# Scores of the banded layers: two heads side by side in the two halves of TensorE's rows

## The chip, the cores and the metric

The kernel runs on one core of a Trainium2 chip, as one launch. The metric is the device time of that core in microseconds (us). The engines are named as in the profile: PE is TensorE's matmul, PEld its weight load, DVE VectorE, ACT ScalarE, POOL GpSimd, SP SyncE, which issues most DMAs. L12 is line 12 of the kernel.

## The reference

A stack of four layers on 1024 image tokens and 256 context tokens of width 1024: windowed attention, latent attention, a gated recurrence, and windowed attention again. The change touches the two layers with windowed attention (0 and 3, here "banded"). There 16 query heads of 64 dimensions share 4 key heads; a block of 128 queries sees three blocks of 128 keys round it and all 256 context keys:

```python
logits = jnp.einsum('bqkgd,bjkd->bkgqj', q_b, k_b).astype(jnp.float32) * scale
p = sink_softmax(jnp.where(mask, logits, NEG_INF), sink_l)
return jnp.einsum('bkgqj,bjkd->bqkgd', p.astype(v_b.dtype), v_b)
```

Context queries (layer 0 alone) see the context keys only. Inputs and outputs are float32.

## The kernel before

To keep float32 accuracy at the rate of the rounded type float32r, each operand is split into a rounded part ("hi") and the rest ("lo"), and products of parts are summed in PSUM. Projections take three products (hi hi, hi lo, lo hi).

A banded layer (`layer_a`) first makes keys and values, then works through units: a group g of four heads that share a key head, by a tile t of 128 queries, 40 units in layer 0 (2 context tiles and 8 image tiles a group) and 32 in layer 3. Queries and keys lie in DRAM (`qd`, `kd`) as four slabs: even and odd dimensions (32 rows each) of hi, and the same of lo. `load_group` (L862) fetches for a group the keys, the four slabs stacked to 128 rows (tile `ks`, 128 x 1280), and the values. `load_q` (L870 to 878) fetches a unit's queries twice: stacked in the same order, and with hi and lo exchanged (tile `qT`, 128 x 2 x 4 x 128). A score product over 128 rows with the first copy gives hi hi + lo lo, with the second hi lo + lo hi.

`stage_s` (L898 to 932) makes the scores of a unit. For each of the four heads it takes a PSUM tile `w` (two buffers), multiplies queries (weights, 128 x 128) with image keys (384 columns, 256 at the two edge tiles, none for context tiles) and with 256 context keys, two products each. Then POOL puts the sink in, DVE adds the mask and takes the maximum (L921), ACT takes the exponential (L923), and for two heads together DVE inverts the sums and POOL scales (L928, L930). `fill(n)` lets n matmuls of the projections of later heads (generator `pq`) follow each head. `stage_pv` (L934 on) turns the probabilities of the unit before with PE transposes (L90), splits them and multiplies them with the values; at its end the result is multiplied with the gate `zin` on POOL (L966) and written out. `made_for` draws the projections that a load needs. `proj_z` makes the gates by way of tile `zs`.

All matmuls go through `mm` (L87), so their lines are one; the tile names tell them apart: `w<-ks,qT` are the scores, `n<-hh,wzh` and the like projections, `n<-ph,v` and `n<-pl,v` the value products, `n<-raw,cs` the conditioning vectors of the next layer, four tiles of 32 columns of the array side by side.

Each engine runs its queue in order. The order in a queue isn't the program's: the framework's scheduler sorts instructions by priority (place in the program) and by when a simulated timeline finds them ready, with waits put in for buffers.

Of the kernel before, what the change touches and what calls it, by code (L numbers as in the profile page):

```python
# [9 lines left out]
F32 = mybir.dt.float32  # L10
F32R = mybir.dt.float32r
BF16 = mybir.dt.bfloat16  # L12
AF = mybir.ActivationFunctionType
ALU = mybir.AluOpType
# [5 lines left out]
NLAT = 1024  # L20
NCTX = 256
T = NLAT + NCTX
# [9 lines left out]
def as32(ap):  # L32
    return ap.bitcast(F32)
# [31 lines left out]
class Dit:  # L65
# [652 lines left out]
    def layer_a(self, i, hpool, hT, hs):  # L718
        nc, ins, P = self.nc, self.ins, self.P
# [3 lines left out]
        qd = [self.pd.tile([4, 128, T], F32, name=f"qd{i}_{g}") for g in range(4)]  # L723
        kd = self.pd.tile([4, 128, T], F32, name=f"kd{i}")
# [29 lines left out]
        for n, t in enumerate(self.order(i - 1)):  # L754
            norm[1](n + 2)
            ps = self.psn()
# [10 lines left out]
            if n == 1:  # L767
                self.run_late()
                qp = self.pool("qp", hs)
# [17 lines left out]
        p2 = self.pool("p2", os_)  # L787
        mask = p2.tile([128, 1152], BF16, name="mask")
        nsink = p2.tile([128, 16], F32, name="nsink")
# [3 lines left out]
        p3 = self.pool("p3", os_)  # L793
# [4 lines left out]
        def piece(w, c, t0, m):  # L798

            hh, hl = hT  # L800
            ps = self.psn()
            ts = slice(t0, t0 + m)
            for k in range(8):
                for x, (a_, b_) in enumerate(((w.wh, hh), (w.wh, hl), (w.wl, hh))):
                    self.mm(ps[:, 0:m], a_[:, k, c], b_[:, k, ts], k == 0 and x == 0, k == 7 and x == 2)
                    yield ps
# [14 lines left out]
        def proj_z(x, pieces):  # L821

            w = P["z", x]
            for t0, m in pieces:
                for ps in piece(w, slice(0, 128), t0, m):
                    yield
                zs = qp.tile([128, 512], F32, name="zs", bufs=2)
                nc.scalar.activation(out=zs[:, 0:m], in_=ps[:, 0:m], func=AF.Tanh, scale=0.5)
                nc.vector.scalar_tensor_tensor(out=zs[:, 0:m], in0=zs[:, 0:m], scalar=1.0, in1=ps[:, 0:m],
                                               op0=ALU.add, op1=ALU.mult)  # L830
                nc.sync.dma_start(out=zd[x * 128:(x + 1) * 128, t0:t0 + m], in_=zs[:, 0:m])
                made.add(("z", x, t0))
# [17 lines left out]
        def made_for(kind, xs, t):  # L850

            for x in xs:
                while (kind, x, t * 128 // 512 * 512) not in made:
                    next(pq)


        fs, fp = (5, 5, 5, 2), (2, 2, 2, 2, 1)
# [2 lines left out]
        st = {}  # L860

        def load_group(g):  # L862
            ks = p2.tile([128, T], F32R, name="ks", bufs=2)
            for p in range(4):
                nc.sync.dma_start(out=as32(ks[32 * p:32 * p + 32]), in_=kd[p, 32 * g:32 * g + 32, :])
            v2 = p2.tile([128, NT, 128], F32R, name="v2", bufs=2)
            nc.sync.dma_start(out=as32(v2), in_=vd[g].rearrange("(t p) d -> p t d", p=128))
            grp[g] = (ks, v2)

        def load_q(u):  # L870
            g, t = units[u]
            made_for("q", (g,), t)
            q = p2.tile([128, 2, 4, 128], F32R, name="qT", bufs=2)
            for x in range(2):
                for p in range(4):
                    nc.sync.dma_start(out=as32(q[32 * p:32 * p + 32, x]),
                                      in_=qd[g][(p + 2 * x) % 4, :, t * 128:(t + 1) * 128].rearrange("(h i) t -> i h t", i=32))
            st[u] = {"qT": q}

        def load_z(u):  # L880
            g, t = units[u]
            made_for("z", (2 * g, 2 * g + 1), t)
            z = p2.tile([128, 2, 128], F32, name="zin", bufs=2)
            nc.sync.dma_start(out=z, in_=zd[g * 256:(g + 1) * 256, t * 128:(t + 1) * 128]
                              .rearrange("(a p) t -> p a t", p=128))
            st[u]["z"] = z
# [11 lines left out]
        def stage_s(u, fill):  # L898
            g, t = units[u]
            qT = st[u]["qT"]  # L900
            ks = grp[g][0]
            s0, mo, kbs = cols(t)
            n = 768 - s0
            nl = 512 - s0
            lsum = p3.tile([128, 4], F32, name="lsum", bufs=2)
            nm = p3.tile([128, 4], F32, name="nm", bufs=2)
            rl = p3.tile([128, 4], F32, name="rl", bufs=2)
            pr = []
            for j in range(4):
                ps = self.psw()  # L910
                if nl:
                    kk = slice(kbs[0] * 128, kbs[0] * 128 + nl)
                    for x in range(2):
                        self.mm(ps[:, s0:512], qT[:, x, j, :], ks[:, kk], x == 0, x == 1)
                for x in range(2):
                    self.mm(ps[:, 512:768], qT[:, x, j, :], ks[:, NLAT:T], x == 0, x == 1)
                p = p3.tile([128, 641], F32, name="p", bufs=8)
                sink = nsink[:, 4 * g + j:4 * g + j + 1]
                nc.gpsimd.tensor_scalar(out=p[:, n:n + 1], in0=sink, scalar1=1.0, scalar2=1.0, op0=ALU.mult, op1=ALU.mult)

                nc.vector.tensor_tensor_reduce(out=p[:, 0:n], in0=ps[:, s0:768], in1=mask[:, mo:mo + n], scale=1.0,  # L921
                                               scalar=sink, op0=ALU.add, op1=ALU.min, accum_out=nm[:, j:j + 1])
                nc.scalar.activation(out=p[:, 0:n + 1], in_=p[:, 0:n + 1], func=AF.Exp, scale=-1.0, bias=nm[:, j:j + 1],  # L923
                                     accum_out=lsum[:, j:j + 1])
                pr.append(p)
                fill(fs[j])
                if j % 2:
                    nc.vector.reciprocal(out=rl[:, j - 1:j + 1], in_=lsum[:, j - 1:j + 1])  # L928
                    for y in (j - 1, j):
                        nc.gpsimd.tensor_scalar(out=pr[y][:, 0:n], in0=pr[y][:, 0:n], scalar1=rl[:, y:y + 1], scalar2=0.5,  # L930
                                                op0=ALU.mult, op1=ALU.mult)
            st[u].update(pr=pr, kbs=kbs)

        def stage_pv(u, fill, end=False):  # L934
            g, t = units[u]
            pr, kbs = st[u]["pr"], st[u]["kbs"]
            load_z(u)
            v2 = grp[g][1]
            po = self.psn()
            nk = len(kbs)  # L940
            prev = None

            def pv(b, ph, pl):
                self.mm(po, v2[:, kbs[b], :], ph, b == 0, False)
                self.mm(po, v2[:, kbs[b], :], pl, False, b == nk - 1)

            for b in range(nk):
                pt = self.psn()
                for j in range(4):
                    self.tr(pt[:, j * 128:(j + 1) * 128], pr[j][:, b * 128:(b + 1) * 128])  # L950
                ph = p3.tile([128, 512], F32R, name="ph", bufs=2)
                pl = p3.tile([128, 512], F32R, name="pl", bufs=2)
                self.split(ph, pl, pt, "act", "dve")
                fill(1 if end else fp[b])
                if prev:
                    pv(*prev)
                prev = (b, ph, pl)
            pv(*prev)
            up = p3.tile([64, 512], F32, name="up", bufs=1)
            nc.scalar.activation(out=up, in_=po[64:128, :], func=AF.Copy)  # L960
            o = p3.tile([128, 2, 128], F32, name="o", bufs=2)
            pv_ = po[0:64, :].rearrange("p (a b t) -> p b a t", b=2, t=128)
            uv = up[:, :].rearrange("p (a b t) -> p b a t", b=2, t=128)
            for b in range(2):
                nc.vector.tensor_tensor(out=o[64 * b:64 * b + 64], in0=pv_[:, b], in1=uv[:, b], op=ALU.add)
            nc.gpsimd.tensor_tensor(out=o, in0=o, in1=st[u]["z"], op=ALU.mult)  # L966
            nc.sync.dma_start(out=od[g * 256:(g + 1) * 256, t * 128:(t + 1) * 128]
                              .rearrange("(a p) t -> p a t", p=128), in_=o)
            del st[u]

        load_group(0)
        made_for("q", (0,), qtiles[-1])
        made_for("z", (0,), qtiles[-1])
        load_q(0)
        load_q(1)
        nu = len(units)
        nq = len(qtiles)
# [4 lines left out]
        def fill(n):  # L982
            for _ in range(n):
                next(pq, None)
        early = 3 if i == self.depth - 1 else 1
        last = nu - 7
        for s in range(nu + 1):
# [20 lines left out]
            if s == nu - early:  # L1008
# [5 lines left out]
                fs, fp = (4, 3, 3, 0), (0, 2, 0, 0, 0)  # L1014
# [1073 lines left out]
```

## Time and profile before

| | us |
|---|---|
| median of 3 runs | 3014.71 (3012.68 to 3015.23) |
| the profiled execution | 3015.6 |
| its span, first to last instruction | 3013.8 |
| PE busy in it | 2825.1 (94%) |
| DVE, POOL, ACT busy | 1631.5, 1297.6, 1246.6 |
| first banded layer's units | about 167 to 640 |
| last banded layer's units | about 2532 to 2935 |

Busy time of PE is the time in which at least one matmul is under way by the profile. A matmul's length there holds its way through the array, so that consecutive ones overlap: what one costs is the distance from its start to the next start. The timeline joins like instructions that follow one another (x8) and gives the first one's start. Its columns are start, length, engine, line, operation, output and inputs, rows*columns of the array, shape, count, and in brackets the idle time before with what ended it.

### The profile page before, as it was taken

What the parts mean: (1) busy time and instruction counts of PE and PEld (TensorE: products, weight loads), DVE (VectorE), ACT (ScalarE), POOL (GpSimd) and SP (SyncE); (2) the same over time, 40 slices, a digit from 0 to 9 for tenths busy, and PEclk for the clock granted to TensorE, in tenths of its full rate; (3) what the DMA queues carried; (4) which work ended last, traced back from release to release, by engine and by line L of the source; (5) the groups of instructions that cost most, each with busy time, mean ns of one, the idle gap of its engine ahead of it and who ended that gap; (6) DMA issues with size and microseconds to landing.
All of it is one profiled execution on the core that took longest, in us unless ns stands there. A gap on an engine that the chain in (4) does not pass through costs nothing. (4 is left out here: it accounts for less than half of the span.)

```text
span 3013.8 us, 49186 instructions
## 1 busy us (share of the span) xinstructions
PE 2825.1 (94%) x17272; PEld 2450.8 (81%) x17272; DVE 1631.5 (54%) x3491; ACT 1246.6 (41%) x2625; POOL 1297.6 (43%) x1543
## 2 busy tenths in 40 slices
PE   6999999899999999999899999998997989999898
PEld 4888888678877788888787788998896788888777
DVE  5356666555522566666456644444465743666662
ACT  2245555543311455555433323331233422555662
POOL 4555555545661011000454231345554536656652
PEclk9999999999999999999999999999999999999999
DMA  8455463644255211111443443997686546444433
GB/s 269 146 164 158 139 177 113 216 121 133 80 193 174 75 37 36 34 36 33 128 141 114 136 146 122 301 290 246 225 274 231 186 126 185 123 117 140 146 101 111
DMA packets 460856, 446.33 MB, mean 148 GB/s; under 512 B 39394, under 2 KB 394234, under 8 KB 460610
## 3 DMA queue, kind: packets, MB, share of 16 engines
q1 hardware_dynamic: 456016, 440.40, 47.1%
q8 instruction: 137, 2.24, 0.3%
q10 hardware_dynamic: 4162, 2.14, 0.3%
q0 software_dynamic: 432, 0.66, 0.1%
q14 instruction: 109, 0.89, 0.1%
HBM read 308.19 MB, written 135.53 MB: 147 GB/s over the span
## 5 line engine op out<-in xcount | busy, mean ns | idle before, releaser
L104 DVE TENSOR_TENSOR pl<-n,ph 128x512 fp32r<-128x512 f32 x488 | 327.5, 686 | 135.8 <-ACT ph L95 117.7
L95 ACT ACTIVATE ph<-n 128x512 fp32r<-128x512 f32 x488 | 284.3, 597 | 214.6 <-PE n L90 169.4
L87 PE MATMUL n<-ph,v 128*128 128x256 f32 (+1 forms) x992 | 293.1, 338 | 22.6 <-ACT ph L95 16.8
L921 DVE CUSTOM_DVE_ANT_0 p<-w,mask,nsink 128x640 f32<-128x640 f32 (+2 forms) x288 | 225.0, 806 | 145.1 <-PE w L87 106.4
L87 PE MATMUL n<-wh,hh 128*128 128x256 f32 x960 | 281.6, 294 | 19.7 <-DVE sg L1752 13.4
L90 PE MATMUL n<-ident,p 128*128 128x128 f32 x1952 | 291.9, 276 | 3.4 <-DVE eo_t L290 1.2
L87 PE MATMUL n<-wl,hh 128*128 128x256 f32 x960 | 278.6, 290 | 2.3 <-DVE wl L104 2.3
L923 ACT ACTIVATE p<-p,nm 128x641 f32<-128x641 f32 (+2 forms) x288 | 220.8, 768 | 139.1 <-DVE nm L921 112.1
L87 PE MATMUL n<-wh,hl 128*128 128x256 f32 x960 | 278.0, 290 | 0.0
L90 PEld LDWEIGHTS n<-ident,p 128*128 128x128 f32 x1952 | 236.9, 143 | 37.3 <-ACT p L1288 2.8
L930 POOL TENSOR_SCALAR p<-p,rl 128x640 f32<-128x640 f32 (+2 forms) x288 | 212.0, 749 | 114.8 <-DVE rl L928 111.2
L87 PE MATMUL n<-pl,v 128*128 128x512 f32 (+1 forms) x656 | 238.1, 363 | 7.8 <-DVE pl L104 6.8
L1339 POOL TENSOR_TENSOR o<-o,z 128x256 f32<-128x256 f32 x40 | 30.4, 759 | 438.6 <-ACT o L1338 235.1
L87 PEld LDWEIGHTS n<-wh,hh 128*128 128x128 f32 x960 | 190.1, 198 | 25.3 <-DVE sg L1752 15.0
L87 PEld LDWEIGHTS n<-ph,v 128*128 128x128 f32 x992 | 175.1, 190 | 42.4 <-ACT ph L95 26.5
L87 PE MATMUL w<-ks,qT 128*128 128x256 f32 (+1 forms) x1088 | 197.9, 308 | 1.5 <-DMA qT<-qd 0.7
L87 PEld LDWEIGHTS n<-wl,hh 128*128 128x128 f32 x960 | 190.2, 198 | 3.3 <-DVE wl L104 3.0
L87 PEld LDWEIGHTS n<-wh,hl 128*128 128x128 f32 x960 | 190.1, 198 | 0.3
L87 PEld LDWEIGHTS w<-ks,qT 128*128 128x128 f32 x1088 | 173.3, 189 | 18.6 <-DVE nm L921 5.2
L104 POOL TENSOR_TENSOR wl<-raw,wh 128x1024 fp32r<-128x1024 f32 x42 | 106.3, 2535 | 117.3 <-DVE wh L97 98.5
L87 PEld LDWEIGHTS n<-pl,v 128*128 128x128 f32 x656 | 125.0, 191 | 26.4 <-DVE pl L104 18.4
L87 PE MATMUL n<-hh,wh 128*128 128x512 f32 (+1 forms) x336 | 123.6, 368 | 5.9 <-DVE mod L402 5.9
(341 smaller groups left out, 7312.0 us busy)
## 6 DMA issues: line engine op xcount, KB each, us to landing
raw<-in_l_w_ada_dram SPq DMA_DIRECT2D x96, 512.0 KB
raw<-in_l_w_in_dram SPq DMA_DIRECT2D x80, 512.0 KB
qT<-qd SPq DMA_DIRECT2D x576, 64.0 KB
raw<-in_l_w_out_dram SPq DMA_DIRECT2D x32, 512.0 KB
vd<-v SPq DMA_DIRECT2D x60, 256.0 KB
xd<-xt SPq DMA_DIRECT2D x30, 512.0 KB
od<-o SPq DMA_DIRECT2D x112, 128.0 KB
go<-od SPq DMA_DIRECT2D x28, 512.0 KB
```

The costliest lines, as they stand in the source:

```text
L87: self.nc.tensor.matmul(out, lhsT, rhs, start=start, stop=stop)
L90: self.nc.tensor.transpose(out, in_, self.ident)
L95: nc.scalar.activation(out=out, in_=in_, func=AF.Copy)
L104: e.tensor_tensor(out=lo, in0=src, in1=as32(hi), op=ALU.subtract)
L921: nc.vector.tensor_tensor_reduce(out=p[:, 0:n], in0=ps[:, s0:768], in1=mask[:, mo:mo + n], scale=1.0, scalar=sink, op0=ALU.add, op1=ALU.mi ...
L923: nc.scalar.activation(out=p[:, 0:n + 1], in_=p[:, 0:n + 1], func=AF.Exp, scale=-1.0, bias=nm[:, j:j + 1], accum_out=lsum[:, j:j + 1])
L930: nc.gpsimd.tensor_scalar(out=pr[y][:, 0:n], in0=pr[y][:, 0:n], scalar1=rl[:, y:y + 1], scalar2=0.5, op0=ALU.mult, op1=ALU.mult)
L1339: nc.gpsimd.tensor_tensor(out=o, in0=o, in1=z, op=ALU.mult)
```

## The change

`stage_s` takes the heads in pairs and both `w` buffers at once. Each head has 64 rows of the array (even and odd dimensions of one part), the first of the pair rows 0 to 63, the second rows 64 to 127, and takes three products (hi hi, hi lo, lo hi) for each stretch of keys, in turn with the other head's; lo lo is left out. `load_q` puts the second head of a pair into the upper 64 rows and fetches each part once. `load_group` puts the keys' hi and lo side by side and the same keys into both halves, so `ks` doubles. To make room, `zs`, `zin` and `o` have one buffer instead of two.

```diff
-                zs = qp.tile([128, 512], F32, name="zs", bufs=2)
+                zs = qp.tile([128, 512], F32, name="zs", bufs=1)
...
-            ks = p2.tile([128, T], F32R, name="ks", bufs=2)
-            for p in range(4):
-                nc.sync.dma_start(out=as32(ks[32 * p:32 * p + 32]), in_=kd[p, 32 * g:32 * g + 32, :])
+            ks = p2.tile([128, 2, T], F32R, name="ks", bufs=2)
+            for y in range(2):
+                for b in range(2):
+                    nc.sync.dma_start(out=as32(ks[64 * y + 32 * b:64 * y + 32 * b + 32]),
+                                      in_=kd[b::2, 32 * g:32 * g + 32, :].rearrange("x i t -> i x t"))
...
-            q = p2.tile([128, 2, 4, 128], F32R, name="qT", bufs=2)
-            for x in range(2):
-                for p in range(4):
-                    nc.sync.dma_start(out=as32(q[32 * p:32 * p + 32, x]),
-                                      in_=qd[g][(p + 2 * x) % 4, :, t * 128:(t + 1) * 128].rearrange("(h i) t -> i h t", i=32))
+            q = p2.tile([128, 2, 2, 128], F32R, name="qT", bufs=2)
+            for y in range(2):
+                for b in range(2):
+                    for x in range(2):
+                        nc.sync.dma_start(out=as32(q[64 * y + 32 * b:64 * y + 32 * b + 32, x]),
+                                          in_=qd[g][b + 2 * x, :, t * 128:(t + 1) * 128]
+                                          .rearrange("(h y i) t -> y i h t", y=2, i=32)[y])
...
-            z = p2.tile([128, 2, 128], F32, name="zin", bufs=2)
+            z = p2.tile([128, 2, 128], F32, name="zin", bufs=1)
...
-            for j in range(4):
-                ps = self.psw()
-                if nl:
-                    kk = slice(kbs[0] * 128, kbs[0] * 128 + nl)
-                    for x in range(2):
-                        self.mm(ps[:, s0:512], qT[:, x, j, :], ks[:, kk], x == 0, x == 1)
-                for x in range(2):
-                    self.mm(ps[:, 512:768], qT[:, x, j, :], ks[:, NLAT:T], x == 0, x == 1)
...
+            for j0 in (0, 2):
+                pss = [self.psw() for _ in range(2)]
+                parts = [(s0, 512, kbs[0] * 128)] if nl else []
+                for c0, c1, k0 in parts + [(512, 768, NLAT)]:
+                    kk = slice(k0, k0 + c1 - c0)
+                    for x, (a, b) in enumerate(((0, 0), (0, 1), (1, 0))):
+                        for y in range(2):
+                            r = slice(64 * y, 64 * y + 64)
+                            self.mm(pss[y][:, c0:c1], qT[r, a, j0 // 2, :], ks[r, b, kk], x == 0, x == 2)
+                for y in range(2):
+                    j = j0 + y
...
+                    fill(fs[j])
+                nc.vector.reciprocal(out=rl[:, j0:j0 + 2], in_=lsum[:, j0:j0 + 2])
...
-            o = p3.tile([128, 2, 128], F32, name="o", bufs=2)
+            o = p3.tile([128, 2, 128], F32, name="o", bufs=1)
```

## Rows read from the trace of the kernel before

**Rows 1.** The page's first part: busy time, share of the span, instructions.

```profile
PE 2825.1 (94%) x17272; PEld 2450.8 (81%) x17272; DVE 1631.5 (54%) x3491; ACT 1246.6 (41%) x2625; POOL 1297.6 (43%) x1543
```

**Rows 2.** Stretches: from:to, length, busy us of PE, PEld, DVE, ACT, POOL; clock, DMA.

```profile
166.00:560.00 394.00, 388.58 (x2390) 333.14 (x2383) 249.57 (x606) 222.44 (x488) 224.74 (x354) 1.00 0.50 149
560.00:640.00 80.00, 66.71 (x409) 50.75 (x408) 49.31 (x121) 47.45 (x93) 46.17 (x65) 0.86 0.67 206
...
2840.00:2935.00 95.00, 81.70 (x444) 66.93 (x443) 61.49 (x137) 63.87 (x128) 61.45 (x88) 0.96 0.46 136
```

**Rows 3.** Timeline of PE: start us, length us (first to last end), instruction, xcount.

```profile
356.68 1.34 PE L87 MATMUL w<-ks,qT 128*128 128x384 f32 x8
357.85 0.60 PE L90 MATMUL n<-ident,p 128*128 128x128 f32 x4
```

**Rows 4.** Groups by shape, whole span, PE: xcount, busy us, mean ns, idle, releasers.

```profile
L87 PE MATMUL w<-ks,qT 128*128 128x256 f32 x704 | 134.1, 285 | 0.8 <-DMA qT<-qd 0.4 <-DVE nm L921 0.3
...
L87 PE MATMUL w<-ks,qT 128*128 128x384 f32 x384 | 104.5, 351 | 0.7 <-DMA qT<-qd 0.2 <-DVE nm L921 0.2
```

**Rows 5.** Timeline of PE round tiles of 32 columns in the first banded layer.

```profile
277.41 0.39 PE L87 MATMUL n<-hh,wql 128*128 128x512 f32 x1
277.63 0.39 PE L87 MATMUL n<-hh,wqh 128*128 128x512 f32 x1
277.95 0.64 PE L87 MATMUL n<-raw,cs 128*32 128x256 f32 x8
278.52 0.50 PE L87 MATMUL n<-hl,wqh 128*128 128x512 f32 x1
278.86 0.40 PE L87 MATMUL n<-hh,wql 128*128 128x512 f32 x1
```

**Rows 6.** Timeline of the weight loads (PEld) in the same stretch.

```profile
277.95 0.16 PEld L87 LDWEIGHTS n<-raw,cs 128*32 128x32 f32 x8 [0.35 <-issue]
278.52 0.19 PEld L87 LDWEIGHTS n<-hl,wqh 128*128 128x128 f32 x1 [0.41 <-issue]
```

**Rows 7.** Timeline of PE round sixteen tiles of 32 columns.

```profile
413.55 1.07 PE L87 MATMUL n<-raw,cs 128*32 128x256 f32 x16
414.55 0.50 PE L87 MATMUL w<-ks,qT 128*128 128x256 f32 x2
```

**Rows 8.** Groups by shape, whole span, weight loads (PEld).

```profile
L87 PEld LDWEIGHTS w<-ks,qT 128*128 128x128 f32 x1088 | 173.3, 189 | 18.6 <-DVE nm L921 5.2 <-issue 1.5 <-DVE eo_t L289 0.4
...
L87 PEld LDWEIGHTS n<-raw,cs 128*32 128x32 f32 x768 | 20.0, 116 | 41.7 <-DMA raw<-in_l_w_ada_dram 15.0 <-issue 14.7 <-DVE eo_t L303 1.7
```

**Rows 9.** Timeline of PE round a transpose of 36 rows, third layer.

```profile
1877.71 0.27 PE L90 MATMUL n<-ident,s 128*128 128x128 f32 x1
1877.92 0.25 PE L1620 MATMUL n<-ident,s 36*128 36x36 f32 x1
1878.10 0.39 PE L87 MATMUL n<-wh,hh 128*128 128x256 f32 x1
1878.32 0.28 PE L87 MATMUL n<-wl,hh 128*128 128x256 f32 x1
1878.43 0.28 PE L87 MATMUL n<-wh,hl 128*128 128x256 f32 x1
```

**Rows 10.** Timeline of PE: the first and the last interrupted run of a head.

```profile
185.78 0.84 PE L87 MATMUL w<-ks,qT 128*128 128x256 f32 x5
186.47 0.40 PE L87 MATMUL n<-pl,v 128*128 128x512 f32 x1
186.70 0.51 PE L87 MATMUL w<-ks,qT 128*128 128x256 f32 x3
...
2927.79 0.52 PE L87 MATMUL w<-ks,qT 128*128 128x256 f32 x3
...
2928.38 0.28 PE L87 MATMUL w<-ks,qT 128*128 128x256 f32 x1
```

**Rows 11.** Tile zin: what ended its engine's idle time (us, times).

```profile
  DMA zin<-zd: 5.1, 2
```

More of the change, by code (lines that the diff above doesn't have):

```diff
@@ L908, in stage_s @@
             pr = []
-            for j in range(4):
-                ps = self.psw()
-                if nl:
-                    kk = slice(kbs[0] * 128, kbs[0] * 128 + nl)
-                    for x in range(2):
-                        self.mm(ps[:, s0:512], qT[:, x, j, :], ks[:, kk], x == 0, x == 1)
-                for x in range(2):
-                    self.mm(ps[:, 512:768], qT[:, x, j, :], ks[:, NLAT:T], x == 0, x == 1)
[L917 to L931, printed above, removed]
@@ new lines, in stage_s @@
+            for j0 in (0, 2):
[9 more added lines that the diff above has]
+                    j = j0 + y
+                    p = p3.tile([128, 641], F32, name="p", bufs=8)
+                    sink = nsink[:, 4 * g + j:4 * g + j + 1]
+                    nc.gpsimd.tensor_scalar(out=p[:, n:n + 1], in0=sink, scalar1=1.0, scalar2=1.0, op0=ALU.mult,
+                                            op1=ALU.mult)
+                    nc.vector.tensor_tensor_reduce(out=p[:, 0:n], in0=pss[y][:, s0:768], in1=mask[:, mo:mo + n], scale=1.0,
+                                                   scalar=sink, op0=ALU.add, op1=ALU.min, accum_out=nm[:, j:j + 1])
+                    nc.scalar.activation(out=p[:, 0:n + 1], in_=p[:, 0:n + 1], func=AF.Exp, scale=-1.0,
+                                         bias=nm[:, j:j + 1], accum_out=lsum[:, j:j + 1])
+                    pr.append(p)
+                    fill(fs[j])
+                nc.vector.reciprocal(out=rl[:, j0:j0 + 2], in_=lsum[:, j0:j0 + 2])
+                for y in (j0, j0 + 1):
+                    nc.gpsimd.tensor_scalar(out=pr[y][:, 0:n], in0=pr[y][:, 0:n], scalar1=rl[:, y:y + 1], scalar2=0.5,
+                                            op0=ALU.mult, op1=ALU.mult)
```

## The prediction

> **What bounds the kernel now.** I read the page's first part first: TensorE is busy for 94% of the span and no other engine for more than 54% [rows 1]. Busy time alone does not say that it streams, since matmuls overlap, so the second view is the table by stage: in the main stretch of the first banded layer PE is busy for 388.6 of 394 us, while at the two ends, where the projections that fill its gaps have run out, it is idle for 13.3 of 80 us and 13.3 of 95 us [rows 2]. The third is the pace inside the score products. Eight of them, two heads of 4 x (384+256) columns, follow one another from 356.68 to 357.85, 1.17 us for 2560 columns, 0.457 ns a column, with the next weights loaded meanwhile [rows 3]. The clock is at its upper level, 2.4 GHz (granted 1.00), in this stretch [rows 2]. So a banded layer is bound by how long TensorE's own sequence takes, and what the change does to that sequence is nearly all of its price. The fourth view counts what it touches: 704 score products of 256 columns and 384 of 384 columns [rows 4], 704x256 + 384x384 = 327,680 columns, 149.8 us at 0.457 ns.
>
> **Part 1: fewer columns in time.** Before, a head takes two full-array products for each stretch of keys; after, three products of 64 rows, and two heads lie in the two halves of the rows. If both halves stream at once, two heads need 3 column passes where they needed 4: 149.8 x 3/4 = 112.4 us, a gain of **37.4 us**. The trace has no two products in different rows, so this is not shown; what it has is four 32-column tiles side by side: eight such products with a whole visit of the mode take 0.57 us and sixteen take 1.00 us [rows 5, 7], hence 0.43 us for eight more, 0.215 us for four of 256 columns together. A 512-column product at the same place takes 0.23 us (277.41 to 277.63) [rows 5]. Tiles beside one another in columns do run together, and I take the same for rows.
>
> **Part 2: going in and out of the half-height mode.** Every other product round these uses the whole array, so each unbroken run of the new products is entered and left once. The trace shows what such a visit costs, in two places. (a) Tiles of 32 columns: the 512-column product starts at 277.63, the tiles at 277.95, 0.32 us later instead of 0.23: 0.09 us of draining. The weight load starts only then, not ahead (277.95, after 0.35 us idle, put down to issue) [rows 5, 6]. On the way out the load again starts with its product at 278.52, and the product after that comes at 278.86, 0.34 us later instead of 0.23: 0.11 us for a load of 128 columns that nothing hides [rows 5, 6]. In all 277.63 to 278.86 is 1.23 us, of which two products of 0.23 and two groups of 0.215 are work: the visit costs 1.23 - 0.46 - 0.43 = 0.34 us. Its loads on the way in have 32 columns, 116 ns each, where the new ones have 128 columns, 189 ns [rows 8]; 0.07 us more is exposed, **0.41 us**. (b) A transpose of 36 rows among full-height work, which is the same kind of step: transpose, 36-row transpose and two 256-column products take from 1877.71 to 1878.43, 0.72 us, where four steps of the neighbours' 0.12 us would be 0.48: **0.24 us**, with ten such transposes in the trace [rows 9]. These are the two ends. I take 0.40, next to (a), because there as here long products stand on both sides whose loads were hidden; in (b) the loads are those of transposes.
>
> The Trainium skill, "TensorEngine Tiling (Array Packing)", section Key Properties, says that changing the tiling mode, not just the tile, drains TensorE. That agrees with the 0.09 us of rows 5; the page gives no figure, and without the rule the sum below would be the gain of part 1 alone.
>
> **How many visits.** 72 units (a group of heads by 128 tokens: 40 in the first layer, 32 in the last) have two pairs of heads each: 144 visits at least, since between two pairs both w buffers must be emptied and other products lie there. PE's order is made by the framework's scheduler, and it breaks runs. Over the whole timeline I counted 58 places where other products stand between two products of one head, the first in the run that begins at 185.78 and the last in that from 2927.79 [rows 10]: the value products of the previous unit come in as they become ready. (The scores form 233 runs in all; runs broken between two heads I leave out, since the new pair is issued together.) The new groups will be interrupted for the same reason, so 144 + 58 = 202 visits; 144 is the low end, 144 + 92 = 236 the high one (if breaks between heads, 92 with the 58, stay too).
>
> **Part 3: what is moved and made single.** Each q value is loaded once instead of twice (the tile has half the elements, still eight DMAs a unit on SP); keys are loaded twice (ks doubles, 8 loads in all). Score products waited 0.4 + 0.2 us for qT, so I put this at nothing [rows 4]; if the cover went, the row says tenths of a us. A pair now takes both w buffers at once, so the next pair waits for the second DVE read; score loads waited 5.2 us for these reads in all [rows 8]. From nothing to another 5 us: nothing taken, since the other products lie between pairs. With one zin buffer the load of a unit's gate waits on SP for POOL's product of the unit before, and behind it stand SP's raw and qT loads; POOL waited 5.1 us for zin in two places [rows 11]. No row shows zs or o waiting. From a us or two below nothing (less traffic) to 10 us for all three; I take 0 because these queues are not the bound, and keep +10 in the range.
>
> **Sum.** 202 x 0.40 = 80.8 us of visits against 37.4 us gained: +43.4. Twelve of the 72 units begin in the two ends where PE idles [rows 2]; half of their share is hidden: 43.4 x 12/72 x 0.5 = 3.6. Net **+40 us** on the profiled execution, whose span is 3013.8 and own time 3015.6, so 3055; the median of the runs is 0.9 below that execution, which I leave. Ends of this case: 144 x 0.24 - 37.4 = -3 and 236 x 0.41 - 37.4 + 10 = +69, that is 3013 to 3085. The turning point is 37.4/202 = 0.185 us a visit.
>
> **Rivals.** *The visit is cheap (faster).* If the half-height products drain the array but the loads run ahead across the change, a visit costs two drains, 0.09 + 0.09; with unbroken pairs 144 x 0.18 - 37.4 = -11, 3004; without any cost 2978. It decides below 0.185 us a visit. For it: a run's first load needs half of the rows only, where the tiles of rows 5 stood over all of them. Against: the loads start with their products, not ahead, both on the way in and on the way out [rows 6], and the incoming full-height load needs both halves.
>
> *Weight loads are not hidden inside the mode (slower).* A pair then carries two loads of 0.11 us [rows 5] one after the other, 0.22 us a pair, more than 256 or 384 columns take: 128 pairs x 6 x 0.22 + 16 x 3 x 0.22 = 179.5 us, 29.7 more than before instead of 37.4 less. That is 67 us on top: +111 before cover, about 3120. The four narrow loads that start together do not look serial [rows 6], which speaks against it. The Trainium skill, "TensorE: Matmul & The Clock Gate", Part 3 (The mechanism), lets a load overlap products in flight only where its rows differ; by that rule a half's next load would wait for the half's product, which comes to this rival's size. The trace does not bear it out for the whole array, where 512-column products on the same rows follow at 0.23 us [rows 5].
>
> *The halves do not run side by side (the change does not do what it says).* Then three passes for each head: 149.8 x 1.5 = 224.7, +75 and +81 of visits: about 3165.
>
> **How the numbers follow.** Forecast (+40, its own range 3013 to 3085) 0.65; cheap visit 0.16 (0.10 near 3004, 0.06 near 2978); loads not hidden 0.10; halves not side by side 0.09. The scheduler's new order may move any of them by some us. A range of 3000 to 3125 leaves out 2978, 3165 and the worse part of the loads' case, nearly 2 in 10. A measurement of this kernel tells 0.2%, 6 us, from no change. Slower by more than that: nearly all of the forecast, 0.57, and the two slow rivals, 0.19, 0.76; faster 0.16; within 0.2% 0.08.
>
> **What would show it.** In the profile after, PE's timeline shows pairs of 64*128 products that start a few ns apart and six such pairs in 0.88 us (forecast), 1.3 us (loads) or 1.76 us (one after the other). The start of a run stands 0.09 us later than the pace before it, its first load starts with it, and so on the way out. Between 144 and 236 runs. DVE's, ACT's and POOL's busy times in these layers stay as they are. I am wrong if the loads of the new runs begin before the product ahead of them has ended, or if the stretches of the banded layers do not grow by about 22 us (first) and 18 us (last).

## The result and the profile after

| | before | after |
|---|---|---|
| median, us | 3013.91 (3012.68 to 3015.23) | 3109.16 (3103.70 to 3119.28) |
| ratio, 95% interval | | 1.0314, 1.0296 to 1.0332 |
| profiled execution: time / span, us | 3015.6 / 3013.8 | 3104.25 / 3102.2 |
| first banded layer, from the start of its first score product to the end of its last, us | 467.4 | 517.3 |
| last banded layer, the same | 401.5 | 442.8 |
| runs of score products with nothing between | 233 | 250 |

The change costs 95 us where 40 were forecast. The two banded layers grow by 49.9 and 41.3 us, 91.2 together; the span grows by 88.4, so nothing was lost elsewhere. The mean granted clock is the same, 0.976 before and 0.975 after. Of e10 below, one of four executions took 4292 us at a granted clock of 0.61 and is left out of its ratio. The first part of the page after, the line of busy times (engine, us, share, instructions):

```profile
PE 2935.2 (95%) x17816; PEld 2478.9 (80%) x17816; DVE 1632.0 (53%) x3491; ACT 1244.8 (40%) x2625; POOL 1296.1 (42%) x1543
```

Against [rows 1] PE is busy for 110 us more, and DVE, ACT and POOL as long as before: all of it is TensorE's own sequence. The same line of code in the groups by shape (xcount, busy us, mean ns, idle before and its releasers), PE and then PEld:

```profile
L87 PE MATMUL w<-ks,qT 64*128 64x256 f32 x1056 | 156.4, 300 | 4.3 <-DMA qT<-qd 3.4 <-DVE nm L931 0.9
...
L87 PE MATMUL w<-ks,qT 64*128 64x384 f32 x576 | 126.4, 376 | 1.5 <-DVE nm L931 1.4
...
L87 PEld LDWEIGHTS w<-ks,qT 64*128 64x128 f32 x1632 | 188.5, 188 | 77.8 <-issue 51.5 <-DVE nm L931 13.4 <-DMA qT<-qd 4.1
```

Before, the two shapes were busy for 134.1 and 104.5 us [rows 4]; after for 156.4 and 126.4, though the two heads of a pair were to share each pass. And where the loads of before had run ahead (1.5 us put down to issue in [rows 8]), those of after stand idle for 51.5 us with nothing to wait for. The view of what tile qT's instructions waited for (us, times) counts the places, before and then after. It adds up the idle time of PE and of PEld before these instructions, and the two overlap where a product waits with its load; the lines put down to issue are PEld's alone:

```profile
  DVE nm L921: 5.7, 20
  issue: 1.5, 3
```

```profile
  issue: 51.5, 176
  DVE nm L931: 15.7, 38
```

176 times a run of score products begins with a load that starts late, by 0.29 us each: the half-height mode is entered there. That was forecast. What was not forecast is how the products stand inside the runs. PE's timeline after, at two places of the first layer (start, length, instruction, xcount):

```profile
267.96 0.39 PE L87 MATMUL n<-hh,wzl 128*128 128x512 f32 x1
268.28 1.32 PE L87 MATMUL w<-ks,qT 64*128 64x256 f32 x12
269.53 0.51 PE L87 MATMUL n<-ph,v 128*128 128x512 f32 x1
269.87 0.39 PE L87 MATMUL n<-pl,v 128*128 128x512 f32 x1
...
322.36 0.98 PE L87 MATMUL w<-ks,qT 64*128 64x256 f32 x6 [0.93 <-DVE nm L931]
323.26 0.50 PE L87 MATMUL n<-ph,v 128*128 128x512 f32 x1
323.70 0.97 PE L87 MATMUL w<-ks,qT 64*128 64x256 f32 x6
324.60 0.51 PE L87 MATMUL n<-pl,v 128*128 128x512 f32 x1
```

At 322.36 six products of 256 columns take 0.90 us to the next product, 0.15 us each with the visit in it: they follow one another, because all six belong to one head, so to one half of the array. The other head's six come at 323.70, in a visit of their own. At 268.28 twelve, a whole pair, take 1.25 us; six pairs side by side take 0.91 (below). The code issues the two heads in turn, but in most places they run one behind the other. By the start times, of 250 runs 63 are six products of which none starts beside another, and 50 are twelve of which few do; 43 of these 50 have the pattern of starts that e7 below shows, where one head's six are queued ahead of the other's. 26 runs are a single product. Only 80, most of them five to seven products long, go in pairs throughout. In all, 348 of the 1632 products start within 30 ns of the one before, so 43% of them run in pairs.

### The profile page after: what moved, and what is told of

Read it like the earlier page. It is cut to its first block, busy times and chain, and to the rows that moved or that the text cites. A ratio compares the mean times of both kernels' runs of the same rounds, so it can differ in the third digit from the quotient of the medians.

```text
span 3102.2 us, 50083 instructions
## 1 busy us (share of the span) xinstructions
PE 2935.2 (95%) x17816; PEld 2478.9 (80%) x17816; DVE 1632.0 (53%) x3491; ACT 1244.8 (40%) x2625; POOL 1296.1 (42%) x1543
## 5 line engine op out<-in xcount | busy, mean ns | idle before, releaser
L87 PEld LDWEIGHTS w<-ks,qT 64*128 64x128 f32 x1632 | 188.5, 188 | 77.8 <-issue 51.5
L87 PE MATMUL w<-ks,qT 64*128 64x256 f32 (+1 forms) x1632 | 244.4, 327 | 5.8 <-DMA qT<-qd 3.4
L87 PE MATMUL n<-pl,v 128*128 128x512 f32 (+1 forms) x656 | 246.4, 376 | 2.0 <-DVE pl L104 1.3
L975 POOL TENSOR_TENSOR o<-o,zin 128x256 f32<-128x256 f32 x72 | 54.5, 757 | 197.9 <-issue 97.1
```

Of the source, the lines that this page charges most:

```text
L87: self.nc.tensor.matmul(out, lhsT, rhs, start=start, stop=stop)
```

## What the experiments were to tell apart

Theory: the visits cost what was forecast, and the rest of the loss is the order; the change itself takes away the two free w buffers that an alternating order needs. Rivals: a visit is dearer than 0.40 us; halves do not stream side by side; the single buffers of zs, zin and o cost time. All ratios are to the kernel before on the same chip. "In runs" is the sum of the intervals from the start of each score product to the start of the next product of any kind; "paired" the share that starts within 30 ns of a neighbour; "DVE waits" are idle time put down to DVE's read of a w buffer, of PE alone unless PEld is named.

| kernel | median us | ratio, interval | runs | paired | in runs us |
|---|---|---|---|---|---|
| before | 3013.91 | | 233 | 0 | 177.9 |
| after | 3109.16 | 1.0314, 1.0296 to 1.0332 | 250 | 43% | 237.6 |
| e5 bound before | 3051.48 | 1.0095, 1.0078 to 1.0112 | 147 | 0 | 185.8 |
| e6 bound pair | 3064.41 | 1.0140, 1.0123 to 1.0157 | 148 | 87% | 168.2 |
| e7 bound, head after head | 3104.10 | 1.0272, 1.0256 to 1.0288 | 147 | 40% | 228.5 |
| e8 bound, full height | 3095.68 | 1.0243, 1.0225 to 1.0261 | 146 | 0 | 246.8 |
| e9 waits for both buffers | 3097.86 | 1.0260, 1.0234 to 1.0286 | 212 | 65% | 192.7 |
| e10 order of after, full height | 3078.34 | 1.0192, 1.0164 to 1.0221 | 248 | 0 | 250.3 |
| e11 waits, with priority | 3062.76 | 1.0140, 1.0113 to 1.0166 | 147 | 86% | 166.9 |
| e12 before with priority | 3022.22 | 1.0011, 0.9998 to 1.0024 | 178 | 0 | 174.3 |

### e1 to e3: the pair in one block of the scheduler

```
                with self.tc.tile_critical():
                    for c0, c1, k0 in parts + [(512, 768, NLAT)]:
...
```

e2 has the loop over the two heads outside the others in the same block; e3 has r = slice(0, 128).

> The changed kernel, with the twelve products of a pair of heads bound into one block for the scheduler: on PE they lie together and the two heads alternate, in 144 runs instead of 250. Theory (order): the loss came from the order, one head's products after the other's (few of the 1632 products overlap) and from runs that were broken more often than forecast. Then the score columns take 149.8 x 3/4 = 112 us, 144 visits at 0.41 us cost 59 us, together 171 us against 150: about +20 us against the kernel before, near 3035. Rival (the mode itself): the halves hinder each other or their weight loads are exposed whatever the order; then only 106 visits fall away, 43 us, and the time stays at about 3066 or above. Rival (buffers): the single zs, zin and o buffers and the pair's two w buffers cost the time; then it stays near 3109.

> As the block of e1, but inside it all six products of the first head, then the six of the second: half-height products with nothing beside them. Order theory: nothing overlaps, 149.8 x 1.5 = 225 us of columns and the same 144 visits, 59 us: +134 us against before, about 3148, 112 us above e1. If the halves gave nothing even when alternated, it equals e1.

> As the block of e1 with alternating heads, but every product takes all 128 rows of queries and keys, so the half-height mode is never entered (the scores are then sums over two heads: that part of the computation is changed). 225 us of columns and no visits: by the order theory +75 us, about 3089. Against e2 it differs by the 144 visits alone: 59 us at 0.41 us each, 35 us at 0.24 us.

Measured 3413.46 (ratio 1.1305, 1.1285 to 1.1324), 3503.81 (1.1604) and 3488.30 us (1.1546): every expectation missed by hundreds of us. The weight loads of e1, by shape:

```profile
L87 PEld LDWEIGHTS w<-ks,qT 64*128 64x128 f32 x1632 | 152.6, 228 | 297.3 <-issue 297.2
```

Ahead of the 144 runs the loads stand idle for 297 us, and PE itself for 248 us. So the totals say nothing on the change. What can be read is what stands inside the blocks of e1: paired 99%, in runs 213.9 us, against 284.5 head after head (e2) and 347.5 at full height (e3). The mean granted clocks are 0.93, 0.91 and 0.94, so these are not to be set beside the rest. e5 to e8 bind the pair by other means.

### e4: the single buffers alone

```
-                zs = qp.tile([128, 512], F32, name="zs", bufs=2)
+                zs = qp.tile([128, 512], F32, name="zs", bufs=1)
...
```

The same for zin and o, on the kernel before.

> The kernel before with only zs, zin and o reduced to one buffer. Order theory and the forecast: no change, within 0.2% of before. Buffer rival: up to the whole difference, +10 us at the upper end of the forecast's bound, more if the rival is right.

Measured 3019.55 us, ratio 1.0002 (0.9989 to 1.0015): no change. On the kernel before, the forecast's 0 for them stands, and its +10, a ratio of 1.0033, lies outside the interval.

### e5 to e8: the pair bound without a block

The products of a pair are chained in the order in which they are issued, have priority in the scheduler, and the first waits for DVE's reads of both w buffers; e5 does that to the kernel before, whose heads it takes in pairs for it, e6 to the changed one.

```
+                                 first = prev is None
+                                 prev = self.behind(m, prev)
+                                 if first:
+                                     for d in self.reads:
+                                         self.tc.add_manual_dep(prev, d.name, ...)
```

e7 has the loop over the two heads outside the others, e8 r = slice(0, 128).

> The kernel before, with the eight full-height products of two heads chained in the scheduler's order, raised in priority and made to wait for the two DVE reads before them: 147 runs instead of 233, no block with waits round it. It is the base for e6 to e8, which have the same binding. The products are the same, so by every theory it stays near before, within some 15 us either way through the new order alone.

> The changed kernel with the binding of e5: twelve half-height products a pair, the heads in turn, 148 runs. Order theory: 112 us of columns against 150 and 148 visits at 0.40 us, +22 us above e5 and far below the changed kernel, near 3035. Rival (the mode itself is dearer than forecast whatever the order): it stays 60 us or more above e5.

> As e6, but the six products of the first head and then the six of the second, 147 runs. If TensorE took them strictly one after another, +112 us above e6. From the runs of this shape in the changed kernel (1.54 us inside a run of twelve against 1.09 us of an alternating one) it lets the second head start early: +0.45 us for 96 pairs and +0.35 us for 32, about +55 us above e6, +75 above e5.

> As e6, but all twelve products over 128 rows, so the half-height mode is never entered and nothing can overlap (scores are sums over two heads: that part of the computation is changed), 146 runs. 225 us of columns and no visits: +75 us above e5, by every theory; it gives the pace of full-height products in the same order. A visit then follows from e6: (e6 - e5 + 37) / 148.

e5 misses its expectation: it is 0.95 points, 29 us, above before where at most 15 were expected (the cause is taken up with e12), and the 3035 expected for e6 misses with it. e6 is 0.45 points, 13 us, over e5, where 22 were expected and 60 or more by the rival, and 1.74 points below after: with the same tiles, the same DMAs and the same mode, order and number of runs alone make some 50 us. PE's timeline of e6 at a pair of 256 columns and the loads there:

```profile
275.00 0.39 PE L88 MATMUL n<-hh,wzh 128*128 128x512 f32 x1
275.31 0.98 PE L88 MATMUL w<-ks,qT 64*128 64x256 f32 x12
276.22 0.50 PE L88 MATMUL n<-pl,v 128*128 128x512 f32 x1
276.56 0.39 PE L88 MATMUL n<-ph,v 128*128 128x512 f32 x1
276.79 0.39 PE L88 MATMUL n<-pl,v 128*128 128x512 f32 x1
```

```profile
275.31 0.78 PEld L88 LDWEIGHTS w<-ks,qT 64*128 64x128 f32 x12 [0.35 <-issue]
276.22 0.19 PEld L88 LDWEIGHTS n<-pl,v 128*128 128x128 f32 x1
```

This is the pair as forecast. The run starts 0.31 us after a product of 0.23, with its load; twelve products take 0.91 us to the next start, where the same twelve of after took 1.25; then 0.34 us instead of 0.23 on the way out. In the start times the two of a pair lie 3 or 4 ns apart, and pairs follow at 115 ns (171 for 384 columns), with the first pair at 220 and the last at 206. So a visit is 0.10 going in, 0.11 coming out, and 0.10 and 0.09 inside, 0.40 us. By the times of whole kernels, the sum that the expectation of e8 names gives (13 + 37) / 148 = 0.34 us.

e7 costs 1.32 points more than e6, 40 us: the order inside a pair, with the number of runs unchanged. e8, at full height with no mode, is 1.48 points above e5, 44 us, for half as many columns again (74.9 us at the pace of [rows 3]; in runs 61.0 more). Both are smaller than expected (55 and 75 us). For e8, part of the added time falls where e5's PE stood idle: it is idle for 192.3 us of its profiled span, e5 for 206.9. What else makes the differences is open.

### e10: the order of after, without the mode

```
-                            r = slice(64 * y, 64 * y + 64)
+                            r = slice(0, 128)
```

> The changed kernel with every score product over all 128 rows instead of a half (so the scores of a pair are sums over both heads, part of the computation is changed), three products a head as in the changed kernel, no half-height mode and no two products at once; the scheduler's order stays as broken as in the changed kernel (248 runs). Columns 149.8 x 1.5 = 224.7 us, 75 more than before, and the same 28 us of waits between them: if the visits of the changed kernel cost 0.40 us each (99 us) and its overlap saved 36 of those 225, this one is about 60 to 75 over the kernel before, 3075 to 3090, and 20 to 35 below the changed kernel. Rival (visits cost nothing there, the columns that run one after the other are the whole loss): it is not below the changed kernel, 3109 or more.

It is 1.92% above before, 58 us, a little less than expected, and 1.22 points, 37 us, below after, though it takes 12.7 us more in runs. The view by shape of its loads:

```profile
L87 PEld LDWEIGHTS w<-ks,qT 128*128 128x128 f32 x1632 | 251.2, 189 | 23.0 <-DMA qT<-qd 4.9 <-DVE o L974 2.5 <-DVE nm L931 2.2
```

The 51.5 us put down to issue are gone with the mode. So in after the visits cost more than all the overlap that its order leaves (93.9 against 65 us in the account below): streaming all three products of every head through the whole array one after another costs less. That the columns are the whole loss falls.

### e9, e11 and e12: why the order is what it is

e9 adds only a dependence on both reads, e11 adds the priority to it, e12 is the kernel before with the priority alone.

```
+                             for d in reads:
+                                 self.tc.add_manual_dep(getattr(m, "ins", m), d.name, ...)
```

> The changed kernel with one thing added: the products of a pair depend on the DVE reads of both w buffers of the pair before, so that both are free when the first of the twelve may start. Nothing binds them to one another, and they have no priority. In the order that the scheduler then makes, most pairs alternate between the two heads, in 212 runs where the changed kernel has 250. Theory (the changed kernel lost its overlap because its two w buffers come free one after the other, which lets the scheduler put one head behind the other): 212 visits at 0.40 us are 85, against 37 us gained, +47 over the kernel before, less about 11 that other idle time gives back: between 3050 and 3065, and the score products take about 130 us of columns where they took 189. Rival (the chain and the priorities of the bound kernels did it, not the buffers): no less than 3090.

> As the run that waits for both reads, with priority for the pair's products in the scheduler as well, and no chain between them: 147 runs, nearly all of them of twelve alternating products. Same theory: 147 visits at 0.40 us are 59, against 37 gained: +21 over a kernel before that is bound in the same way. If what the binding cost there (29 us) lies in the chain, this one is near 3035; if it lies in the wait or the priority, it is near the 3064 of the bound pair. In both cases its score products take about 115 us of columns.

> The kernel before with priority for its score products in the scheduler alone, no chain and no wait added (178 runs of score products where the kernel before has 233). It tells what of the 29 us of the bound kernel before is the priority's: 3040 or more if all of it, within 6 us of the kernel before if the chain and the wait made it. If fewer interruptions were worth something at full height, it would come out below the kernel before; I expect no gain.

e9 was half right. With both buffers free at once the scheduler does alternate more: 65% paired, 45 us less in runs than after. But the kernel came out 0.54 points below after, not the 1.5 to 2.0 expected; by its time alone it falls to the rival. The view of tile w (us, times, PE and PEld added up as above) says where part of the gain went; here its line for DVE's reads in e9, then in e5, then in e6:

```profile
  DVE nm L942: 60.3, 88
```

```profile
  DVE nm L941: 28.3, 47
```

```profile
  DVE nm L947: 36.2, 73
```

Before, these waits were 5.7 us in the same view (all of them in tile qT's instructions). PE's own part in e9 stands in the groups by shape:

```profile
L88 PE MATMUL w<-ks,qT 64*128 64x256 f32 x1056 | 109.3, 294 | 11.4 <-DMA qT<-qd 6.3 <-DVE nm L942 4.9
L88 PE MATMUL w<-ks,qT 64*128 64x384 f32 x576 | 92.4, 381 | 16.6 <-DVE nm L942 13.8 <-DMA qT<-qd 2.6
```

So PE itself stands 18.7 us for DVE's reads in e9, in 32 places, where in after it was 2.3 us in 4. It is busy for 2879.8 us, 55 less than in after, with 46 more idle, of which these 16 more are the largest part that has one cause; qT's loads make 5.5 more, and the rest is spread over inputs of other products. A head's read takes 0.88 us, and the products of both next heads now stand behind the second one. So the two buffers cost either way: released one after the other, the heads are mostly put one after the other and do not overlap; waited for together, PE waits. The expectation for e9 priced the first and took the second for free.

e11 is e6 without its chain, and gives the same time: the chain costs nothing. But against e9 it has only the priority more, and that is worth 1.20 points, 36 us: 147 runs instead of 212, 86% paired instead of 65%, and 9.6 us of DVE waits instead of 18.7. So the rival of e9 was right about the priority and wrong about the chain. No run gives the changed kernel the priority without the wait, so the two are not told apart further. e12 is within 0.2% of the kernel before: there priority alone neither costs nor gives. What e5 loses to the kernel before, 0.95 points, is therefore mostly the wait for both reads together with the taking of two heads at once that needs it (0.84 points above e12, 25 us). PE's busy time is the same in both, 2836.0 us; e5 has 20 us more idle, and 9.4 us of DVE waits against 1.6.

## Why the prediction was wrong in size

The score work in the two layers, from the start times. Of each visit 0.20 us is taken to lie inside its run, as in e6; the rest (33.1 and 10.8) is what the products ahead of the runs and those behind them take longer than their own pace, less the same in before:

| term | forecast | measured |
|---|---|---|
| columns and the waits between them | -37.4 | 237.6 - 250 x 0.20 - 177.9 = +9.7 |
| visits | 202 x 0.40 = 80.8 | 250 x 0.20 + 33.1 + 10.8 = 93.9 |
| all else in the layers | -3.6 | -12.4 |
| sum | +39.8 | +91.2 |

**The step that failed** stands in brackets in "How many visits": "runs broken between two heads I leave out, since the new pair is issued together". Issued together in the code is not queued together: the two w buffers come free one after the other, and the scheduler put one head behind the other; made to wait for both, it paired more of them (e9, 65% for 43%). That one assumption carried two terms. It cost 47.1 us in the columns: of 224.7 us that three full passes a head take, 112.3 should have been saved by overlap. With the 28.1 us of waits that before had between its products (177.9 - 149.8), an assumption that e10 supports (250.3 - 224.7 = 25.6), after's columns are 187.6 - 28.1 = 159.5 us, so 65 were saved. And it cost 13.1 us in the visits, 250 instead of 202, beyond even the high end of 236.

**Part 3 held in after only because the pairs came apart**: "so the next pair waits for the second DVE read", with nothing taken and 5 us at most. In after PE stands 2.3 us for these reads. Where the order keeps the pair together, the wait and what goes with it cost 25 us (e5 above e12), of which 9.4 are DVE waits by name. The row to read for it was not the 5.2 us that score loads waited [rows 8], which two buffers for one head each had kept small, but how long a read holds its buffer, 0.88 us, beside a pair that needs both.

**Part 1 was right** where the pair is in order: e6 takes 168.2 - 148 x 0.20 = 138.6 us for columns and waits, 47.2 less than e5; its own waits, 26.2 above 112.4, are as before. Halves do stream side by side, which no row before had shown.

**The visit was right**: 0.40 forecast, 0.40 in e6's rows, 93.9/250 = 0.38 as the mean in after, 0.34 by whole kernels (e6, e5). End (a) of part 2, the 32-column tiles [rows 5], was the right row; end (b), the short transposes, was too low. The 0.10 us going in agrees with the Trainium skill, "TensorEngine Tiling (Array Packing)", section Key Properties: a change of the mode drains TensorE.

**The single buffers and the q and key loads** at nothing: right for the buffers (e4); PE waits 3.4 us for qT in after where before it waited 0.7, a few us that the sum left out.

**Tail cover** was put at 3.6 us of gain; what lies outside the score products gave 12.4 back. PE's idle time in the two layers fell from 37.6 to 22.7 us, which fits that PE, being later, finds other inputs ready more often; no run separates it.

**The rivals.** The cheap visit fell (0.40 in e6, against 0.185 as the turning point). Loads that are not hidden fell: pairs at 115 and 171 ns leave no room for two loads of 0.11 us. With it the rule of the Trainium skill, "TensorE: Matmul & The Clock Gate", Part 3 (The mechanism), that a load overlaps products in flight only where its rows differ, is not what the trace of e6 shows. Halves not side by side fell as a property of the chip (e6) and half came true as one of the order: 43% paired.

**What would show it.** Pairs some ns apart, the drain of about 0.09 us and the load that starts with its product all appeared. "Between 144 and 236 runs" and "about 22 us (first) and 18 us (last)" did not: 250 runs, 49.9 and 41.3 us. Two signs could not do their work. Six pairs in 0.88 us held in e6 (1.08 less 0.20 of the visit); most whole pairs of after took 1.54 - 0.20 = 1.34, the figure given for loads that are not hidden, and it was the order. And loads that begin before the product ahead has ended stand already in the rows of before: the load at 277.95 [rows 6] begins while the product from 277.63, 0.39 us long, has not ended by its record [rows 5].

No kernel here beats the one before. With every pair whole the visits alone are 144 x 0.40 = 57.6 us against 37.4 gained; it breaks even at 93 visits, which would want all four heads of a unit in one run and four w buffers where there are two. That was not tried.

## What to carry to other kernels

Count a packing's gain only over products that will stand together in the engine's queue, and look for what could part them: here two output buffers that come free at different times, so that a pair needing both is either queued in halves or waits. Price each change of the array's mode per visit (0.40 us here) and put the visits, as the order will break them, against the columns saved, before any other term. If a scheduler makes the order, make that order a line of the prediction with its own low and high, since one wrong assumption there moved two terms the same way.

## What the runs showed of the hardware

Products queued head after head still overlap in part. In e7 all six products of one head stand ahead of the other's six, 384, 384, 384, 256, 256, 256 columns each, yet 40% start as pairs. PE's timeline of one such run, cut at 263.65, and of the whole run:

```profile
263.02 0.91 PE L88 MATMUL w<-ks,qT 64*128 64x384 f32 x4
```

```profile
263.02 1.61 PE L88 MATMUL w<-ks,qT 64*128 64x384 f32 x12
264.56 0.50 PE L88 MATMUL n<-pl,v 128*128 128x512 f32 x1
```

Four products of 384 columns have started by 263.65, where the first head has three: the fourth is the other head's first, at 263.49 in the records, 7 ns after the third and ahead of three products that stand before it in the program's order. All 96 such runs of e7 start four products of 384 columns ahead of any of 256. So TensorE starts work for the idle half early, but not at once, and "each engine runs its queue in order" does not hold here for the starts of products in the two halves. The run takes 1.54 us, between the 1.08 of an alternating one in e6 and the 1.96 of two heads wholly one after the other (twelve products at 0.457 ns a column, 1.76, and 0.20 of the visit). In after 103 of the 348 pairs stand in runs of twelve that are paired in part, and 228 in the runs that are in pairs throughout; so this is one reason, and the smaller one, why after still saved 65 us of columns.
